# Turning the delta rule's values and queries on the vector engine instead of the tensor engine, in a two-layer hybrid decoder trunk

## The chip, the cores and the metric

The kernel runs on one core of a Trainium2 chip. A core has five engines with instruction streams of their own: the tensor engine (PE, with its weight loads shown apart as PEld), the vector engine (DVE), the scalar engine (ACT), GpSimd (POOL) and the sync engine (SP), which here issues every DMA. The engines meet through semaphores only, and each works through its own instructions in the order in which the program lists them. Compute reads and writes SBUF, 128 partitions wide; the tensor engine writes PSUM, eight banks of 128 x 512 float32. DRAM is reached by DMA.

The metric is the device time of one execution in microseconds (us), as the median of three runs. The profile is one further execution, with its own time.

## The reference

The trunk has two layers over a sequence of 2048 tokens of 1024 channels. Each layer projects its input to all heads at once, runs four heads of a gated delta rule beside four heads of gated linear attention (GLA), gates and mixes the heads, and adds the residual under a LayerNorm. Cut to the delta rule, which the change touches:

```python
dn_qkv = silu(causal_short_conv(concat([dn_q, dn_k, dn_v]), conv_w))   # 4 taps per channel
q = l2norm(cq) * 128 ** -0.5 ;  k = l2norm(ck) ;  v = cv               # per head of 128 channels
g = -exp(a_log) * softplus(dn_a + dt_bias) ;  beta = sigmoid(dn_b)
# per head:  S_t = a_t (I - b_t k_t k_t^T) S_{t-1} + b_t k_t v_t^T ,  o_t = S_t^T q_t    (a_t = exp g_t)
o_dn = head_rms_norm(o_dn, norm_g) * silu(dn_z)
y = concat([o_dn, o_gla]) @ w_out ;  x = layer_norm(alpha * x + y)
```

Everything is float32. The kernel does the delta rule in chunks of 128 tokens: within a chunk a triangular inverse, between chunks a 128 x 128 state S per head.

## The kernel before

**Tiling.** Each layer is done in two halves of 1024 tokens, so there are four passes, called halves below. A half is two blocks of 512 tokens, a block four chunks of 128. A projection of one head is a group of 24 matmuls into one PSUM bank (tag `pj`): the input `xt` and the weights are split into a high and a low part of a rounded float32 type (`xt`, `wh`, `wl`), and high x high, high x low and low x high are summed. Its output has channels on the partitions and the block's 512 tokens along the free axis.

**Where turns are needed.** The delta rule needs some tensors the other way round, with tokens on the partitions. The function `transpose4` makes four tensor-engine transposes of 128 x 128 into a bank with tag `tr` (the names `tr<-ident,...` in the profile, `ident` being the identity matrix). It is called three times per head and block: in `dn_keys`; in `dn_values`, where the convolved values are turned and then scaled per token by the vector engine straight out of PSUM; and in `dn_queries`, where the turned queries serve only the per-token sums of squares, which the scalar engine takes by `sumsq4`. GLA turns its keys the same way, and the very first input too. The layer's input and the attention output are already turned in another way (`turned`): the vector engine transposes 32 x 32 blocks in place (STREAM_TRANSPOSE), and the loads bring the blocks to their places.

**The recurrence.** `dn_rec` goes through the four chunks of a block. Each chunk is a chain over the engines: PE multiplies keys and queries by the state (`ch<-Sd,kq`), DVE forms the right-hand side `rr` from it and the scaled values `vb`, PE applies the inverse (`ch<-rr,m`), ACT or DVE scales that to `vn`, PE makes the state's update and the output (`ch<-vn,m`), DVE updates the state `Sd`. The turned values are first needed in `rr`; the queries' sums of squares only when the block's output is normalised.

**The inverse.** `dn_invert` sends small blocks to DRAM and back twice (`nd`, then `ud`), a round trip of the kind that the change adds; `dn_merge` puts the inverse together on PE.

**What sets the order.** A recorder (class `Recorder`) takes down all operations with their dependences, and a list scheduler with a table of costs chooses the order in which every engine's instructions are written; at the end one line (L433) emits them all, so every row of the profile carries that line, and groups are told apart by tile names. The scheduler takes the ready operation with the smallest key. The key is the operation's place in the program, less a lift. The text `PLAN` lists the stages of a half in program order, with a lift behind a plus sign: `q` and `w` are GLA's projections, `a` and `b` its two parts per pair of heads and block, `d` decays, `k`, `v`, `y` the delta rule's keys, values and queries of a head, `i` and `m` inverse and merge, `r` the recurrence of a head and block, `g` a gate's projection. Operations that two engines can do (`copy`, `scaled`, `subtract`, `product`) go to the one that the scheduler finds free sooner.

**Buffers.** Tiles are taken from a fixed number of slots per tag: three `tr` banks, twenty tiles of tag `m2`, five of `m4`, two raw weight tiles `wr`, three each of `wh` and `wl`. An operation that needs a slot waits until one is free.

Of the kernel before, what the change touches and what calls it, by code (L numbers as in the profile page):

```python
# [14 lines left out]
ALU = mybir.AluOpType  # L15
# [461 lines left out]
def _cost(o, outs, ins):  # L477
# [57 lines left out]
    else:  # L535
# [5 lines left out]
P = 128  # L541
# [3 lines left out]
NC = BLK // P  # L545
# [10 lines left out]

LAST = 1, 2, 3
FIRST = 300
PLAN = ("q0+50 w a00 d1 b00+50 a01 q1 d0+100 a10 b01 d2 k0 v0 b10+50 g4 a11 i0 b11+700 y0+100 k1+500 g5+200 m0 r00 k2 y1 "
        "r01 d3+200 i1 m1+50 v1 k3 g6 r10 y2 i2 m2+500 i3+150 v2+450 v3+100 r20 g7+400 m3+250 r11+950 r21 g0+100 y3+50 r30 r31")  # L560


@with_exitstack
def hymba_trunk(ctx: ExitStack, tc, x, w_in, conv_w, dn_a_log, dn_dt_bias, gla_gate_w2, gla_gate_b,
# [12 lines left out]
    def C(shape, name, dt=F32):  # L577
        return rec.sbuf(shape, name, dt)
# [4 lines left out]
    def small(w):  # L583
        return T([P, w], "s1")
# [21 lines left out]
    m0 = C([P, 32], "m0", U8)  # L606
# [60 lines left out]
    def bc(ap, n):  # L667
        return ap.unsqueeze(2).to_broadcast([ap.shape[0], ap.shape[1], n])
# [5 lines left out]
    subtract, product = partial(combine, ALU.subtract), partial(combine, ALU.mult)  # L674

    def copy(out, a, pool=False):
        calls = [("scalar", "copy", (out, a), {}), ("vector", "tensor_copy", (out, a), {})]
        if pool:
            calls.append(("gpsimd", "tensor_copy", (out, a), {}))
        rec.either(*calls)  # L680

    def scaled(out, a, by):
        rec.either(("scalar", "activation", (out, a, AF.Copy), dict(scale=by)),
                   ("vector", "tensor_scalar", (), dict(out=out, in0=a, scalar1=by, scalar2=None, op0=ALU.mult)))
# [51 lines left out]
    def proj_group(w, xtb):  # L736
        hi, lo = w
        xh, xl = xtb
        acc = PS([P, BLK], "pj")
        for k in range(KT):  # L740
            nc.tensor.matmul(acc, hi[:, k, :], xh[:, k, :], start=(k == 0), stop=False)
            nc.tensor.matmul(acc, hi[:, k, :], xl[:, k, :], start=False, stop=False)
        for k in range(KT):
            nc.tensor.matmul(acc, lo[:, k, :], xh[:, k, :], start=False, stop=(k == KT - 1))
        return acc
# [136 lines left out]
    def load_dec(decd, h, b):  # L882
        dec = T([P, NC, P], "m2")
        nc.sync.dma_start(dec, decd[h * NB + b].rearrange("p (c t) -> p c t", c=NC))
        return dec
# [197 lines left out]
    def conv_silu(acc, grp, tag):  # L1083
        raw = T([P, 515], "raw")
        nc.gpsimd.tensor_copy(raw[:, 0:3], halo[:, grp, :])
        copy(raw[:, 3:515], acc)
        nc.gpsimd.tensor_copy(halo[:, grp, :], raw[:, 512:515])
        y = T([P, BLK], tag)
        scaled(y, acc, cw[:, 36 + grp:37 + grp])
        for k in (2, 1, 0):  # L1090
            nc.vector.scalar_tensor_tensor(out=y, in0=raw[:, k:k + BLK], scalar=cw[:, 12 * k + grp:12 * k + grp + 1],
                                           in1=y, op0=ALU.mult, op1=ALU.add)
        nc.scalar.activation(y, y, AF.Silu)
        return y

    def transpose4(src):
        pt = PS([P, NC, P], "tr")
        for c in range(NC):
            nc.tensor.transpose(pt[:, c, :], src[:, c * P:(c + 1) * P], ident)
        return pt  # L1100

    def across(src):

        half = T([P, 4, NC, 32], "m2")
        nc.vector.transpose(half.pattern(0, [(32, NC), (P, 4), (1, 32)]), src.rearrange("p (c b t) -> p c b t", c=NC, b=4))
        d = DR([4, 32, 4, P], "tp")
        nc.sync.dma_start(d.rearrange("a i b e -> (a i) (b e)"), half.rearrange("p b c i -> p (b c i)"))
        t = T([P, 4, P], "m2")
        for a in range(4):
            nc.sync.dma_start(t[:, a, :], d[a].rearrange("t b e -> b t e"))  # L1110
        return t.pattern(0, [(32, NC), (P, 4), (1, 32)])

    def bc4(ap):
        return ap.unsqueeze(2).unsqueeze(3).to_broadcast([P, NC, 4, 32])

    def blocks(t):
        return t.rearrange("p c (a i) -> p c a i", a=4)

    def sumsq4(pt, dst):
        for c in range(NC):  # L1120
            o, i = T([P, P], "sq", BF16), pt[:, c]
            if len(i.dims) > 1:
                o = o.rearrange("p (a i) -> p a i", a=4)
            nc.scalar.activation(o, i, AF.Square, accum_out=dst[:, c:c + 1])
# [127 lines left out]

    def dn_values(l, h, b, w, xtb, st):
        k = st["b"][b]
        pt = transpose4(conv_silu(proj_group(w, xtb), 8 + h, "m2"))
        if b == 0:
            st["vb"] = T([P, NCH, P], "m4")
        nc.vector.tensor_tensor(out=st["vb"][:, b * NC:(b + 1) * NC, :], in0=pt, in1=bc(k["rk"], P), op=ALU.mult)

    def dn_queries(l, h, b, w, xtb, decd, st):  # L1260
        k = st["b"][b]
        dec = load_dec(decd, h, b)
        qT = conv_silu(proj_group(w, xtb), h, "kq")
        pa = PS([P, NC, P], "tr")
        for c in range(NC):
            cs = slice(c * P, (c + 1) * P)
            nc.tensor.matmul(pa[:, c, :], k["kT"][:, cs], qT[:, cs], start=True, stop=True)
        if b == 0:
            st["at"] = T([P, NCH, P], "m4")
        nc.vector.tensor_tensor(out=st["at"][:, b * NC:(b + 1) * NC, :], in0=pa, in1=dec, op=ALU.mult)  # L1270
        sq_ = small(NC)
        sumsq4(transpose4(qT), sq_)
        nc.vector.tensor_scalar(out=sq_, in0=sq_, scalar1=128.0 * EPS, scalar2=128.0 * EPS * EPS,
                                op0=ALU.mult, op1=ALU.add)
        k["qT"], k["sq"] = qT, sq_
# [121 lines left out]
    for l in range(depth):  # L1397
# [4 lines left out]
        for hf in range(n_half):  # L1402
# [72 lines left out]
            def values(h):  # L1475
                w = load_group(l, V0 + P * h)
                for b in range(NB):
                    dn_values(l, h, b, w, xt[b], dn[h])

            def queries(h):  # L1480
                w = load_group(l, Q0 + P * h)
                for b in range(NB):
                    dn_queries(l, h, b, w, xt[b], decd, dn[h])
# [3 lines left out]
                     "m": lambda h: dn_merge(dn[h]), "r": rec_block}  # L1487
            for step in PLAN.split():
                name, _, ahead = step.partition("+")
# [40 lines left out]
```

## Time and profile before

| | |
|---|---|
| three runs | 2093.4 us median (2091.4 to 2093.82) |
| the profiled execution | 2097.92 us |
| its span, first to last instruction | 2096.2 us, granted tensor clock 0.997 |
| PE busy | 2058.8 us, 98% |
| DVE busy | 1478.2 us, 71% |
| ACT busy | 1159.4 us, 55% |
| POOL busy | 504.9 us, 24% |
| DMA | 249.00 MB, mean 119 GB/s |
| STREAM_TRANSPOSE on DVE, 128 x 512 | 112 of 686 ns |
| `tr<-ident` turns on PE, 128 x 128 | 512 |

Rows of groups read: engine, operation, output<-inputs by tile name, shape, count | busy us, mean ns of one | idle time of the engine just before them, and what ended it. Matmuls overlap, and a row's duration is the time from start to end of one; what a matmul costs the engine is the distance to the next start. A float32 matmul of 128 columns shows as two records, a float32 transpose as one.

### The profile page before, as it was taken

To read this page: it belongs to the slowest core of one execution; us is meant where nothing else is said; L and a number is where in the kernel's file an instruction comes from. 1 tells how busy PE (TensorE), PEld (TensorE's weight loads), DVE (VectorE), ACT (ScalarE), POOL (GpSimd) and SP (SyncE) were. 2 spreads that over 40 slices of the span, in tenths; PEclk is the share of its full clock that TensorE was granted. 3 is DMA by queue.
4 is the path that set the end of the run, shared out by engine and by line. 5 is a ranking of instruction groups with operands and counts; after the bars stand their busy time and mean duration, and the time that the engine had idled before them with its cause. 6 is when DMAs were issued, how large, how long until landed. Compare 5 with 4: busy or idle time off the path is not lost.

```text
span 2096.2 us, 45723 instructions
## 1 busy us (share of the span) xinstructions
PE 2058.8 (98%) x16882; PEld 1742.3 (83%) x16882; DVE 1478.2 (71%) x3349; ACT 1159.4 (55%) x3284; POOL 504.9 (24%) x864
## 2 busy tenths in 40 slices
PE   7999999999999999999999999999999999999998
PEld 7888888888888887787888888878888888877877
DVE  4478787479657778757965777865795577886576
ACT  3677765532557775553266766555227576665520
POOL 3243211012234221111213322210131442211121
PEclk9999999999999999999999999999999999999999
DMA  4232433597223433359623333235962333333692
GB/s 142 74 99 81 126 89 80 144 228 207 72 72 103 113 89 79 94 157 242 177 72 82 99 97 104 76 87 173 235 187 59 90 95 100 93 78 85 176 224 71
DMA packets 334616, 249.00 MB, mean 119 GB/s; under 512 B 64756, under 2 KB 284216, under 8 KB 334392
## 3 DMA queue, kind: packets, MB, share of 16 engines
q1 hardware_dynamic: 334392, 246.08, 44.3%
q8 instruction: 133, 2.18, 0.5%
q14 instruction: 91, 0.75, 0.1%
HBM read 183.01 MB, written 62.98 MB: 117 GB/s over the span
## 4 chain that ended last, share of the span: by engine, by line
PE 86%; DMA 5%; DVE 4%; issue 2%; ACT 2%; POOL 1%; SPq 0%; DVEq 0%; ACTq 0%; POOLq 0%
PE pj L433 68%; PE ch L433 8%; PE tr L433 8%; PE mg L433 2%; DMA m<-zg 2%; DVE tmp L433 1%; DVE m L433 1%; DMA m<-in_w_out_dram 1%; DVE R L433 1%; ACT m L433 1%; DMA m<-xs 1%; SPq L433 0%; DMA m<-in_x_dram 0%; DMA U<-ud 0%; ACT wh L433 0%
## 5 line engine op out<-in xcount | busy, mean ns | idle before, releaser
L433 PE MATMUL pj<-xt,wh 128*128 128x512 f32 x4096 | 1068.2, 401 | 11.7 <-ACT wh L433 6.4
L433 PEld LDWEIGHTS pj<-xt,wh 128*128 128x128 f32 x4096 | 747.2, 189 | 160.8 <-ACT wh L433 8.6
L433 PE MATMUL pj<-xt,wl 128*128 128x512 f32 x2048 | 551.1, 399 | 0.0
L433 PEld LDWEIGHTS pj<-xt,wl 128*128 128x128 f32 x2048 | 373.8, 188 | 69.4 <-issue 0.2
L433 POOL TENSOR_TENSOR s<-s,mhalf 128x4 f32<-128x4 f32 (+2 forms) x80 | 95.5, 1194 | 440.6 <-DVE s L433 431.8
L433 PE MATMUL pj<-wh,xt 128*128 128x256 f32 (+1 forms) x1024 | 194.6, 289 | 1.9 <-ACT xt L433 0.9
L433 PEld LDWEIGHTS pj<-wh,xt 128*128 128x128 f32 x1024 | 162.0, 190 | 3.8 <-ACT xt L433 1.5
L433 ACT CAST wh<-wr 128x1024 fp32r<-128x1024 f32 (+2 forms) x116 | 117.5, 1019 | 83.3 <-PE pj L433 78.3
L433 DVE SCALAR_TENSOR_TENSOR kq<-raw,cw,kq 128x512 f32<-128x512 f32 x192 | 145.6, 759 | 14.6 <-ACT kq L433 9.6
L433 DVE TENSOR_TENSOR wl<-wr,wh 128x512 fp32r<-128x512 f32 (+2 forms) x173 | 122.5, 737 | 17.6 <-ACT wh L433 13.0
L433 PE MATMUL pj<-wl,xt 128*128 128x280 f32 (+1 forms) x512 | 130.6, 288 | 0.0
L433 ACT CAST wh<-m 128x1024 fp32r<-128x1024 f32 (+2 forms) x44 | 36.3, 829 | 155.3 <-DVE m L433 63.7
L433 DVE TENSOR_TENSOR m<-m,m 128x256 f32<-128x256 f32 (+1 forms) x209 | 89.6, 452 | 22.2 <-ACT m L433 8.3
L433 ACT COPY m<-m 64x256 f32<-64x256 f32 (+1 forms) x228 | 89.4, 412 | 18.4 <-DVE m L433 8.4
L433 PEld LDWEIGHTS pj<-wl,xt 128*128 128x128 f32 x512 | 97.6, 191 | 0.3
L433 POOL MEMSET m<- 128x512 f32 (+1 forms) x160 | 78.3, 507 | 52.5 <-PE tr L433 45.4
L433 DVE SCALAR_TENSOR_TENSOR Sd<-Sd,eg,ch 128x128 f32<-128x128 f32 x112 | 38.6, 345 | 71.6 <-PE ch L433 70.8
L433 PEld LDWEIGHTS ch<-Sd,kq 128*128 128x128 f32 x480 | 72.2, 190 | 13.0 <-DVE Sd L433 1.6
L433 PEld LDWEIGHTS ch<-vn,m 128*128 128x128 f32 x496 | 74.5, 191 | 10.3 <-ACT vn L433 0.9
L433 ACT ACTIVATE sq<-tr 128x128 bf16<-128x128 f32 x256 | 67.6, 276 | 22.5 <-PE tr L433 12.6
L433 POOL COPY halo<-raw 128x3 f32<-128x3 f32 x96 | 23.5, 245 | 234.7 <-ACT raw L433 187.9
L433 PE MATMUL ch<-vn,m 128*128 128x128 f32 x496 | 77.6, 276 | 0.4 <-ACT vn L433 0.4
(205 smaller groups left out, 3330.9 us busy)
## 6 DMA issues: line engine op xcount, KB each, us to landing
wr<-in_w_in_dram SPq DMA_DIRECT2D x312, 128.0 KB, 2.8
og<-m SPq DMA_DIRECT2D x64, 256.0 KB, 2.4
m<-decd SPq DMA_DIRECT2D x64, 256.0 KB, 3.5
zg<-m SPq DMA_DIRECT2D x64, 256.0 KB, 2.5
m<-in_w_out_dram SPq DMA_DIRECT2D x128, 128.0 KB, 3.9
m<-og SPq DMA_DIRECT2D x128, 128.0 KB, 4.5
m<-zg SPq DMA_DIRECT2D x128, 128.0 KB, 4.3
wr<-in_w_in_dram SPq DMA_DIRECT2D x26, 512.0 KB, 3.9
```

The costliest lines, as they stand in the source:

```text
L433: getattr(getattr(self.nc, o.eng), o.name)(*[real(a) for a in o.args], **{k: real(a) for k, a in o.kw.items()})
```

## The change

The two calls of `transpose4` in `dn_values` and `dn_queries` become calls of `across`, and the stage table is another one.

```diff
-PLAN = ("q0+50 w a00 d1 b00+50 a01 q1 d0+100 a10 b01 d2 k0 v0 b10+50 g4 a11 i0 b11+700 y0+100 k1+500 g5+200 m0 r00 k2 y1 "
-        "r01 d3+200 i1 m1+50 v1 k3 g6 r10 y2 i2 m2+500 i3+150 v2+450 v3+100 r20 g7+400 m3+250 r11+950 r21 g0+100 y3+50 r30 r31")
+PLAN = ("q0 w a00 d1 b00+50 a01 q1 d0 a10 b01 d2 k0 v0 b10+50 g4 a11 i0 b11+900 y0+100 k1+900 m0 g5+200 r00 y1 k2 "
+        "d3+800 i1 r01 m1+50 v1 r10 y2 i2 m2+600 r11+950 k3 g6 i3+250 m3+250 v2+450 r20+50 g7+400 v3+150 r21+50 g0 y3+200 r30 r31")
...
     def dn_values(l, h, b, w, xtb, st):
         k = st["b"][b]
-        pt = transpose4(conv_silu(proj_group(w, xtb), 8 + h, "m2"))
+        pt = across(conv_silu(proj_group(w, xtb), 8 + h, "m2"))
         if b == 0:
             st["vb"] = T([P, NCH, P], "m4")
-        nc.vector.tensor_tensor(out=st["vb"][:, b * NC:(b + 1) * NC, :], in0=pt, in1=bc(k["rk"], P), op=ALU.mult)
+        product(blocks(st["vb"][:, b * NC:(b + 1) * NC, :]), pt, bc4(k["rk"]))
...
         sq_ = small(NC)
-        sumsq4(transpose4(qT), sq_)
+        sumsq4(across(qT), sq_)
```

`across` stood in the file before and was called by nothing:

```python
    def across(src):
        half = T([P, 4, NC, 32], "m2")
        nc.vector.transpose(half.pattern(0, [(32, NC), (P, 4), (1, 32)]), src.rearrange("p (c b t) -> p c b t", c=NC, b=4))
        d = DR([4, 32, 4, P], "tp")
        nc.sync.dma_start(d.rearrange("a i b e -> (a i) (b e)"), half.rearrange("p b c i -> p (b c i)"))
        t = T([P, 4, P], "m2")
        for a in range(4):
            nc.sync.dma_start(t[:, a, :], d[a].rearrange("t b e -> b t e"))
        return t.pattern(0, [(32, NC), (P, 4), (1, 32)])
```

One vector instruction transposes the sixteen 32 x 32 blocks of all four chunks where they stand. One DMA writes the result to DRAM, 2 KB from each partition, and four DMAs read it back, each 128 runs of 512 bytes, so that the blocks change places. The result lies in SBUF, where the turned tensor lay in PSUM before: the values' scaling now reads two SBUF operands, and `product` lets the scheduler give it to DVE or POOL; the squares of the queries read SBUF. Eight DRAM buffers (tag `tp`) serve the trips in turn, and each call takes two more `m2` tiles and one `tr` bank less.

## The prediction

> **What bounds the kernel now.** I read the page's shares first, then the slices, then the chain that ended last.
>
> ```profile
> span 2096.2 us, 45723 instructions
> PE 2058.8 (98%) x16882; PEld 1742.3 (83%) x16882; DVE 1478.2 (71%) x3349; ACT 1159.4 (55%) x3284; POOL 504.9 (24%) x864
> ...
> PE   7999999999999999999999999999999999999998
> ...
> DMA packets 334616, 249.00 MB, mean 119 GB/s; under 512 B 64756, under 2 KB 284216, under 8 KB 334392
> ...
> PE 86%; DMA 5%; DVE 4%; issue 2%; ACT 2%; POOL 1%; SPq 0%; DVEq 0%; ACTq 0%; POOLq 0%
> ```
>
> PE is busy in every slice but the first and last, and makes 86% of the chain. A busy PE may still be waiting inside an instruction, so I went to the four stretches in which the delta rule runs, one per layer and half.
>
> ```profile
> 127.00:440.00 313.00, 313.00 (x2764) 262.44 (x2763) 227.82 (x576) 203.13 (x639) 66.84 (x125) 1.00 0.41 113
> 636.00:952.00 316.00, 313.23 (x2747) 262.05 (x2746) 227.47 (x573) 202.23 (x635) 72.28 (x129) 1.00 0.41 110
> 1154.00:1469.00 315.00, 310.97 (x2741) 258.70 (x2740) 227.76 (x582) 198.24 (x626) 68.30 (x125) 1.00 0.39 107
> 1671.00:1991.00 320.00, 315.10 (x2747) 263.32 (x2746) 228.68 (x573) 202.00 (x635) 71.06 (x126) 0.99 0.39 106
> sum 1264.00, PE 1252.30 PEld 1046.51 DVE 911.73 ACT 805.60 POOL 278.48; mean PE 313.07 PEld 261.63 DVE 227.93 ACT 201.40 POOL 69.62
> ```
>
> The columns are length, then busy time of PE, PEld, DVE, ACT and POOL, granted clock, DMA share, GB/s. PE idles 1264.0 - 1252.3 = 11.7 us in all four; DVE is busy 911.7 / 1264 = 72%, the DMA engines about 40%. Here PE's own issue rate sets the time, so what leaves PE should leave the span.
>
> **What leaves PE.** The timeline of the first stretch shows a turn inside a run of projection matmuls, and one behind the attention product.
>
> ```profile
> 163.78 1.07 PE L433 MATMUL pj<-xt,wl 128*128 128x512 f32 x4
> 164.70 0.60 PE L433 MATMUL tr<-ident,m 128*128 128x128 f32 x4
> 165.05 0.72 PE L433 MATMUL pj<-xt,wl 128*128 128x512 f32 x2
> ...
> 204.96 1.98 PE L433 MATMUL pj<-xt,wl 128*128 128x512 f32 x8
> 206.77 0.38 PE L433 MATMUL tr<-kq,kq 128*128 128x128 f32 x2
> 206.99 0.60 PE L433 MATMUL tr<-ident,kq 128*128 128x128 f32 x4
> 207.35 0.48 PE L433 MATMUL pj<-xt,wh 128*128 128x512 f32 x1
> ```
>
> First column: start. Four turns inside projections hold PE from 164.70 to 165.05, 0.35 us; neighbours lose nothing visible (the four matmuls before take 164.70 - 163.78 = 0.92 us, 0.23 each). Behind tr<-kq,kq the group takes 206.99 to 207.35, 0.36 us, but without it the last float32 pass would hand over to a projection sooner: its two passes take 0.22 us, 0.11 each, whereas the last of four turns hands over after 0.36 - 3 x 0.11 = 0.03. Removing such a group therefore saves up to 4 x 0.11 = 0.44 us.
>
> The groups of PE bear out the counts:
>
> ```profile
> L433 PE MATMUL tr<-ident,m 128*128 128x128 f32 x256 | 40.1, 287 | 9.3 <-DMA m<-in_x_dram 8.9 <-DVE xt L433 0.4
> L433 PE MATMUL tr<-ident,kq 128*128 128x128 f32 x256 | 38.9, 273 | 0.0
> ```
>
> Two calls x 4 heads x 2 blocks x 4 halves = 64 groups of four go, half from each row; keys, gated attention and the first input keep the other 256 turns. The same place in the built program, PE, the query product of the first head's first block (kq_168 is the query, pj_159 and pj_160 the projections around it); before:
>
> ```order
> L433 MATMUL pj_159<-xt_148,wl_144 128x512 x8
> L433 MATMUL tr_157<-kq_168,kq_175 128x128
> L433 MATMUL tr_155<-ident_63,kq_168 128x128 x4
> L433 MATMUL pj_160<-xt_149,wh_140 128x512
> L433 MATMUL pj_160<-xt_148,wl_143 128x512 x8
> ```
>
> and now:
>
> ```order
> L433 MATMUL pj_159<-xt_148,wl_144 128x512 x8
> L433 MATMUL tr_155<-kq_168,kq_175 128x128 x2
> L433 MATMUL pj_160<-xt_148,wh_140 128x512
> L433 MATMUL pj_160<-xt_149,wh_140 128x512
> L433 MATMUL pj_160<-xt_148,wl_143 128x512 x8
> ```
>
> The turns are gone, the rest stands. Value groups mostly lie among projections, query groups behind the product: 32 x 0.35 + 32 x 0.44 = 11.2 + 14.1 = **25.3 us**, between 64 x 0.35 = 22.4 and 64 x 0.44 = 28.2.
>
> **What comes in its place.** These groups give the prices (count | busy us, mean ns | idle before).
>
> ```profile
> L433 DVE STREAM_TRANSPOSE kq<-m 128x512 f32<-128x512 f32 x112 | 72.8, 686 | 6.1 <-DMA m<-og 5.8 <-DMA m<-xs 0.2
> L433 DVE TENSOR_TENSOR m<-tr,s 128x512 f32<-128x512 f32 x32 | 22.0, 688 | 5.2 <-PE tr L433 4.3 <-POOL m L433 0.5
> L433 DVE TENSOR_TENSOR m<-kq,m 128x512 f32<-128x512 f32 x49 | 33.3, 699 | 15.3 <-DMA m<-zg 10.6 <-ACT m L433 3.7 <-DMA zg<-m 1.0
> L433 POOL TENSOR_TENSOR m<-kq,m 128x512 f32<-128x512 f32 x31 | 46.2, 1502 | 110.9 <-DMA m<-zg 46.3 <-DVE kq L433 32.5 <-PE pj L433 13.2
> L433 DVE TENSOR_TENSOR wl<-wr,wh 128x512 fp32r<-128x512 f32 x158 | 106.0, 702 | 7.3 <-ACT wh L433 6.1 <-DMA decd<-m 0.5
> L433 ACT ACTIVATE sq<-tr 128x128 bf16<-128x128 f32 x256 | 67.6, 276 | 22.5 <-PE tr L433 12.6 <-DVE m L433 9.5
> L433 ACT ACTIVATE sq<-m 128x128 bf16<-128x128 f32 x128 | 39.3, 307 | 66.7 <-DVE m L433 60.7 <-DVE s L433 3.5 <-DVE R L433 1.6
> ```
>
> DVE gets 64 block turns of 512 columns: 64 x 0.686 = 43.9 us. Its 32 products out of PSUM (22.0 us) become products out of SBUF, 28 on DVE (19.6 us by the 699 ns row), 4 on POOL (6.0 us). By the built program's counts the new order also hands 16 weight differences of 512 columns from DVE to POOL, 11.2 us less on DVE (POOL is at 278.5 / 1264 = 22%). DVE's net is 43.9 - 22.0 + 19.6 - 11.2 = +30.3 us, less some copies and scalings that ACT takes; over four stretches that lifts 72% to at most (911.7 + 30.3) / 1264 = 75%. The 128 query squares on ACT read SBUF instead of PSUM: 128 x (307 - 276) = 4.0 us on an engine at 64%. The projections that PE runs meanwhile hide both, so I cost them at nothing; without that cover they would be 34.3 us.
>
> [...]
>
> The transfers add 64 writes of 256 KB and 256 reads of 64 KB on SP, 33.6 MB beside 249; at 40% DMA share that is hidden. What is late is the round trip. Its likeness is the inverse's trip nd:
>
> ```profile
> 229.53 0.37 SPq L433 DMA_DIRECT2D nd<-T  x1
> 230.00 0.53 SPq L433 DMA_DIRECT2D zg<-m  x1
> 232.36 0.38 SPq L433 DMA_DIRECT2D wr<-in_w_in_dram  x1
> 232.80 1.03 SPq L433 DMA_DIRECT2D m<-nd  x2
> ...
> DMA to landing us min/median/max: 2.2/2.7/8.3
> ...
> L433 SPq DMA_DIRECT2D nd<-T x16: 360/388/398, 172.2 to 1886.1; - x16
> ...
> SPq L433 <- DMA nd<-T: 23.4, 12, 3.5
> SPq L433 <- DVE wl L433: 389.4, 90, 27.9
> DVE V L433 <- DMA m<-nd: 3.1, 5, 0.9
> ```
>
> Write to first read 3.3 us, three more issues at about 0.5, landing 2.7: some 7.5 us. The wait falls on whoever reads the result in line. DVE, second value block of the third head (m_11_124 the convolved values, m_10_123 the turned ones, m_4_154 the scaled values); before:
>
> ```order
> L433 SCALAR_TENSOR_TENSOR rr_216<-ch_163,eg_104,m_4_154 128x128
> L433 TENSOR_TENSOR wl_143<-wr_138,wh_140 128x512
> L433 STREAM_TRANSPOSE T_0_204<-U_0_212 128x256
> L433 COPY m_3_129<-T_0_204 32x8x32 x2
> L433 TENSOR_TENSOR m_0_150<-tr_156,s_6_188 128x512
> ```
>
> and now:
>
> ```order
> L433 STREAM_TRANSPOSE m_16_126<-m_11_124 128x4x4x32
> L433 COPY Nd_201<-m_4_120 32x128 x2
> L433 TENSOR_TENSOR wl_145<-wr_138,wh_141 128x512
> L433 STREAM_TRANSPOSE T_0_212<-Nd_201 128x256
> L433 TENSOR_SCALAR vn_222<-ch_163,s_14_196 128x128
> L433 TENSOR_SCALAR m_7_136<-m_7_136,gg_90 128x512
> L433 TENSOR_TENSOR wl_143<-wr_139,wh_140 128x512 x2
> L433 SCALAR_TENSOR_TENSOR rr_224<-ch_163,eg_104,m_4_154 128x128
> L433 COPY V_215<-m_0_150 128x128
> L433 TENSOR_TENSOR m_4_154<-m_10_123,s_4_187 128x512
> ```
>
> The product now stands ten instructions behind its turn, the shortest distance of the 28; it was fed by PSUM. Three differences alone are 2.1 us; with the rest I estimate some 5 us against 7.5, so DVE may stand 2.5 us there, with V's chain queued behind it. The likeness says less: V waited for nd in 5 of 16 places, 3.1 us in all, 0.2 each. At 0.2 the 64 trips cost 12 us of DVE and ACT idling, off PE's path. I take 0 for PE, since values are needed only when their head's recurrence starts.
>
> **The order.** The table adds no instruction; it puts the fourth head's keys and a gate's projection (k3, g6) behind the second head's two recurrence blocks, and v3 behind the third's first, with the weight and decay loads that they issue on SP. So the projections that cover a recurrence's waits are others, and PE's idle places move. It can at best remove the 11.7 us above, and I allow as much the other way; nothing in the trace says which, so 0.
>
> **Sum.** The profiled execution took 2097.92 us around its span of 2096.2; less 25.3 is 2072.6. It lay 4.5 above the runs' median of 2093.4, from which I count: 2093.4 - 25.3 = **2068**. Range: low 2093.4 - 28.2 - 11.7 = 2053; high 2093.4 - 22.4 + 11.7 = 2083, a microsecond added for ACT.
>
> **Rivals.**
> *Vector waits reach PE (slower).* DVE is in line: a product that stands for its trip holds up the recurrence's rr or S behind it. PE has four projections between those steps:
>
> ```profile
> 306.84 0.61 PE L433 MATMUL ch<-Sd,kq 128*128 128x128 f32 x4
> 307.20 1.16 PE L433 MATMUL pj<-xt,wh 128*128 128x512 f32 x4
> 308.21 0.38 PE L433 MATMUL ch<-rr,m 128*128 128x128 f32 x2
> ...
> PE ch L433 <- DVE rr L433: 2.9, 3, 1.9
> ```
>
> That is 308.21 - 307.20 = 1.0 us of cover. With 2.5 us at all 28 products, 28 x 1.5 = 42 us reach PE: 2068 + 42 = **2110**. It decides from 25.3 / 28 = 0.9 us beyond cover per product. For it: that estimate of 2.5. Against: 2.9 us of waiting for rr in the whole trace, and V's 0.2.
> [...]
> *SP makes weights late.* Each trip's reads wait at SP's head for the write, 23.4 / 12 = 2 us by the row, with weight loads behind. Were 13 of the 64 to delay a load by 1 us that PE feels: **2081**. Against: loads already stand 389.4 us for a free buffer, so they run ahead.
> *The turns were free*: PE would wait anyway for the recurrence, and nothing changes, **2093**. Against: 11.7 us idle in 1264.
>
> **Chances.** Forecast 0.72, weights late 0.12, Vector waits 0.09, free turns 0.07. A change within 0.2% (4.2 us) can't be told from none. Faster: 0.72 + 0.12 + 0.01 = 0.85; same: 0.06 + 0.01 = 0.07; slower 0.08. The range 2053 to 2084 leaves out the last two cases and the forecast's tails.
>
> **What would show it.** Right: the groups tr<-ident,kq and tr<-ident,m at 128 each, PE's busy time lower by about 25 us and still 98%, DVE between 1490 and 1510 us, its waits on the trips' reads under 15 us, PE's wait for rr under 5 us. Wrong: PE under 97% in the stretches, long waits of PE for DVE rr or Sd (the second case) or for ACT wh (the third); a block turn far over 686 ns; or a PE as long as before.

## The result, and the profile after

The changed kernel took 2120.7 us in the median (2117.1 to 2127.4), the kernel before 2093.4: a ratio of **1.0133, 95% interval 1.0119 to 1.0146**, so 27 us slower where 25 us faster had been forecast. Its profiled execution took 2127.4 us. The page's head, with the clock of the whole execution below it:

```profile
span 2125.7 us, 45829 instructions
PE 2055.1 (97%) x16626; PEld 1726.5 (81%) x16626; DVE 1485.4 (70%) x3339; ACT 1175.7 (55%) x3328; POOL 536.2 (25%) x894
...
DMA packets 377627, 282.57 MB, mean 133 GB/s; under 512 B 66804, under 2 KB 319032, under 8 KB 377400
```
```profile
core 0: 2125.7 us, clock 0.989
```

The 256 transposes are gone (16882 to 16626 records), and yet PE is busy only 3.7 us less. Three parts explain the span. PE stands idle for 2125.7 - 2055.1 = 70.6 us, before for 37.4: +33.2. The clock that was missing is (1 - 0.989) x 2125.7 = 23.4 us, before (1 - 0.997) x 2096.2 = 6.3: +17.1. What is left, busy time without the clock's share, went from 2052.5 to 2031.7: -20.8. The sum is +29.5, the difference of the two spans. So the gain was there, and more than twice as much was lost in idling and in a lower clock.

The four stretches of the delta rule (columns as in the prediction: length, busy time of PE, PEld, DVE, ACT, POOL, granted clock, DMA share, GB/s):

```profile
126.00:447.00 321.00, 308.67 (x2673) 255.17 (x2672) 226.80 (x573) 204.23 (x644) 73.11 (x131) 0.98 0.47 131
655.00:966.00 311.00, 306.93 (x2680) 253.95 (x2679) 230.31 (x576) 204.64 (x641) 74.44 (x133) 1.00 0.48 134
1172.00:1500.00 328.00, 311.10 (x2667) 256.64 (x2667) 225.19 (x556) 206.16 (x654) 77.86 (x135) 0.97 0.45 126
1707.00:2021.00 314.00, 308.62 (x2683) 255.60 (x2682) 232.07 (x580) 204.10 (x639) 75.21 (x132) 0.99 0.47 133
sum 1274.00, PE 1235.31 PEld 1021.35 DVE 914.37 ACT 819.13 POOL 300.62; mean PE 308.83 PEld 255.34 DVE 228.59 ACT 204.78 POOL 75.16
```

PE's idle time in them grew from 11.7 to 1274.0 - 1235.3 = 38.7 us. Whom PE waited for, and who waited for the trips (total us, times, longest):

```profile
PE ch L433 <- DVE Sd L433: 11.2, 9, 2.3
...
PE pj L433 <- DVE m L433: 6.9, 7, 3.3
PE pj L433 <- ACT wh L433: 6.6, 8, 2.3
...
PE ch L433 <- DVE rr L433: 3.8, 3, 3.2
```
```profile
DVE m L433 <- DMA m<-tp: 25.1, 17, 3.5
DVE V L433 <- DMA m<-nd: 20.1, 5, 6.4
...
ACT sq L433 <- DMA m<-tp: 13.4, 10, 3.2
...
POOL m L433 <- DMA m<-tp: 18.2, 4, 12.8
...
SPq L433 <- DMA tp<-m: 72.3, 37, 3.7
```

PE waits for the state `Sd` 11.2 us (0.4 before) and for `rr` hardly more than before (3.8 against 2.9); for weights on ACT no longer than before (6.6 against 6.4). Three engines wait 56.7 us for the new trips, and the inverse's old trip `nd` is now waited for 20.1 us instead of 3.1, though nothing in it was changed. (For this kernel the profile pairs a wait with the last transfer issued on the semaphore that ended it, so the name of a transfer is inferred.) SP's queue is held at its head for 72.3 us by reads whose write hasn't landed.

The second value block of the first head shows it in one place: SP's queue, then the rows of DVE, ACT, POOL and PE that follow from it (start, length, what; in brackets the idle time before):

```profile
171.02 0.43 SPq L433 DMA_DIRECT2D tp<-m  x1
...
172.02 0.42 SPq L433 DMA_DIRECT2D nd<-T  x1
175.00 2.34 SPq L433 DMA_DIRECT2D m<-tp  x4
177.43 1.90 SPq L433 DMA_DIRECT2D m<-nd  x4
```
```profile
182.42 0.69 DVE L433 TENSOR_TENSOR m<-m,s 128x512 f32<-128x512 f32 x1 [3.50 <-DMA m<-tp]
```
```profile
183.41 0.41 ACT L433 COPY m<-m 64x256 f32<-64x256 f32 x1 [4.45 <-DVE s L433]
```
```profile
183.47 1.80 POOL L433 TENSOR_TENSOR s<-s,mhalf 128x8 f32<-128x8 f32 x1 [6.36 <-DVE s L433]
```
```profile
186.69 0.46 PE L433 MATMUL tr<-m,m 128*32 128x32 f32 x32 [1.28 <-POOL m L433]
187.08 1.66 PE L433 MATMUL pj<-xt,wh 128*128 128x512 f32 x6
190.76 3.69 PE L433 MATMUL pj<-xt,wh 128*128 128x512 f32 x8 [2.03 <-ACT kq L433]
```

From the write's issue at 171.02 to the product at 182.42 the trip lasts 11.4 us. DVE stands 3.5 us for it, ACT and POOL stand for DVE, and PE, four microseconds on, for them: 3.3 us in two pauses. In the 31 places where an engine waited for a trip it lasted 6.6 to 12.6 us from the write's issue, 9.7 in the median.

### The profile page after: what moved, and what is told of

Same layout as the page of the kernel before. It is cut to its first block, busy times and chain, and to the rows that moved or that the text cites. A ratio compares the mean times of both kernels' runs of the same rounds, so it can differ in the third digit from the quotient of the medians.

```text
span 2125.7 us, 45829 instructions
## 1 busy us (share of the span) xinstructions
PE 2055.1 (97%) x16626; PEld 1726.5 (81%) x16626; DVE 1485.4 (70%) x3339; ACT 1175.7 (55%) x3328; POOL 536.2 (25%) x894
## 5 line engine op out<-in xcount | busy, mean ns | idle before, releaser
L433 PEld LDWEIGHTS pj<-xt,wh 128*128 128x128 f32 x4096 | 754.9, 191 | 176.7 <-ACT wh L433 14.2
L433 DVE TENSOR_TENSOR wl<-wr,wh 128x512 fp32r<-128x512 f32 (+2 forms) x156 | 115.0, 764 | 30.9 <-ACT wh L433 24.1
L433 ACT ACTIVATE sq<-m 128x128 bf16<-128x128 f32 x256 | 77.2, 304 | 90.5 <-DVE m L433 71.1
L433 POOL TENSOR_TENSOR wl<-wr,wh 128x512 fp32r<-128x512 f32 (+1 forms) x56 | 77.6, 1390 | 84.3 <-PE pj L433 36.9
L433 PE MATMUL ch<-Sd,kq 128*128 128x128 f32 x480 | 79.5, 282 | 11.5 <-DVE Sd L433 11.2
L433 PEld LDWEIGHTS ch<-vn,m 128*128 128x128 f32 x496 | 74.1, 192 | 17.1 <-ACT vn L433 4.6
```

The source lines that it names most:

```text
L433: getattr(getattr(self.nc, o.eng), o.name)(*[real(a) for a in o.args], **{k: real(a) for k, a in o.kw.items()})
```

## The experiments

Each kernel was timed beside the kernel before on the same chip, which took 2092.0 to 2093.6 us in the median. Ratios are to that, with their 95% interval. The diffs show the deciding lines only, in places shortened; a label behind a line names its run.

### Is it the new table?

e1 is the change with the table of before; e2 is the kernel before, its turns on PE, with the table of the change (the same two lines the other way round).

```diff
-PLAN = ("q0 w a00 d1 b00+50 a01 q1 d0 a10 b01 d2 k0 v0 b10+50 g4 a11 i0 b11+900 y0+100 k1+900 m0 g5+200 r00 y1 k2 "
+PLAN = ("q0+50 w a00 d1 b00+50 a01 q1 d0+100 a10 b01 d2 k0 v0 b10+50 g4 a11 i0 b11+700 y0+100 k1+500 g5+200 m0 r00 k2 y1 "
...
```

> The changed kernel with the stage table of before: the turns go through DRAM, the order is the planner's answer to the old table. Theory 1, the trips' waits: the changed kernel's reader of a turned tensor stands in line on DVE, ACT or POOL until a trip of about 11 us has landed (I had reckoned 7.5), and PE runs dry; the old table has the same trips, so 2095 to 2125 us. Theory 2, the new table: the order of stages costs the time and the turns give what was forecast, so about 2068 us (2060 to 2080). Theory 3, SP's queue: the 320 added DMAs hold up the other loads on SP; as theory 1, 2095 to 2125 us.

> The kernel before with the stage table of the change: turns on PE, no trips. Theories 1 and 3: the table is not the cause, 2085 to 2100 us. Theory 2: the table itself costs some 50 us, 2130 to 2150 us.

Measured: the change with the old table 2152.0 us (ratio 1.0289, 1.0271 to 1.0307), the old turns with the new table 2090.0 (0.9989, 0.9980 to 0.9998). The table isn't the cause: alone it is worth 2 us, and without it the change would be 31 us slower still, which is more than any of the three theories expected.

### What do the trips cost?

Three runs keep the written order of the change, and in all three the readers take a constant tile in place of the turned blocks. e3 and e10 leave out the trip's DMAs as well, e10 the block turns too; e4 keeps both.

```diff
             for o in order:
+                if o.eng == "sync" and any(v.buf.tag == "tp" for v in sum(_operands(o), [])):      # e3, e10
+                    continue
+                if o.eng == "vector" and any(id(v.buf) in halves for v in _operands(o)[0]):        # e10
+                    continue
+                o.args, o.kw = tuple(still(o, a) for a in o.args), {k: still(o, a) for k, a in o.kw.items()}
```

> The changed kernel in its own written order, without its 320 trip DMAs; the readers of the turned tensors (the values' scaling, the queries' squares) read a constant tile of the same shape instead, so values and query norms are left out of the computation. The block turns on DVE stay. Theories 1 and 3: the added waits go, 2062 to 2080 us. Theory 2: the order is unchanged, so 2110 to 2122 us.

> The changed kernel in its own written order with all its trip DMAs, but nobody reads what they bring: the readers of the turned tensors read a constant tile of the same shape (values and query norms are left out of the computation). It takes the waits for the trips away and keeps SP's load. Theory 1: 2065 to 2085 us. Theory 2: 2110 to 2122 us. Theory 3: SP's queue is as full as before, 2105 to 2122 us. Between 2085 and 2105 us both the waits and the queue have a share, which the difference from the run without trips then gives.

> As the run without trip transfers (2083.8 us), and the 64 block turns of the vector engine (0.65 us each, 42 us of it) are left out too, so that nothing of the turn is left but its readers (values and query norms are left out). If the vector engine's added work kept PE from its gain, this run nears the 25.3 us of the forecast below before: 2066 to 2075. If PE, with its transposes gone, only runs into the other waits sooner (the output's and the inverse's trips, casts of weights), it stays at 2079 to 2085.

Measured: without trips 2083.8 us (0.9958, 0.9946 to 0.9971), with the trips' transfers but nobody waiting for them 2107.6 (1.0074, 1.0050 to 1.0098), without trips and turns 2082.8 (0.9953, 0.9938 to 0.9968). So of the 37 us between the change and the run without trips, 13 go to waits for the turned blocks, and 24 to the transfers themselves, whose blocks nobody waits for; e4's interval leaves 5 us either way in this split. The 64 block turns on DVE cost 1 us, which is within the noise: there the forecast, that the projections hide them, held. The run without trips took 4 us more than the 2062 to 2080 expected.

The run without trips also tells why even a free trip doesn't give 25 us. Its head and that of the old turns with the same table:

```profile
span 2081.3 us, 45188 instructions
PE 2036.2 (98%) x16626; PEld 1718.3 (83%) x16626; DVE 1485.0 (71%) x3339; ACT 1175.3 (56%) x3328; POOL 532.6 (26%) x894
```
```profile
span 2086.7 us, 45640 instructions
PE 2055.2 (98%) x16882; PEld 1737.8 (83%) x16882; DVE 1462.4 (70%) x3330; ACT 1156.1 (55%) x3287; POOL 515.0 (25%) x880
```

Their clocks were 0.995 and 0.999. With (1 - clock) x span taken off, PE's work is 2025.8 against 2053.1: 27.3 us less, a little over the 25.3 forecast. But PE idles 45.1 us instead of 31.5, and the clock loses 8.3 more; 5.4 us of the span are left. A PE that arrives sooner can stand at other trips, which in this order end no sooner. Its longest pause after the start, on PE, and what DVE had stood for shortly before (`og` is the trip of the attention output, in the kernel before as well):

```profile
987.72 1.52 PE L447 MATMUL pj<-xt,wh 128*128 128x512 f32 x5 [3.21 <-DVE m L447]
```
```profile
979.37 1.31 DVE L447 STREAM_TRANSPOSE kq<-m 128x512 f32<-128x512 f32 x2 [2.44 <-DMA m<-og]
```

From there DVE works without a pause; only at 986.90 does it come to the instruction that empties the PSUM bank (`m<-m,pj`, 0.68 us), and PE's projection starts when that is done. The two runs share the table but not the written order (that of e3 was laid out for trips), so how much of the idle time is a PE that comes too soon and how much is the order wasn't separated.

### Is it SP's held queue, or readers that were written too early?

e5 is e4 with reads that take their bytes from the input, so that they don't wait for their write. e8 is the change, but the planner (the list scheduler) is told that a trip lasts 3 us longer.

```diff
+                if o.eng == "sync" and any(v.buf.tag == "tp" for v in _operands(o)[1]):            # e5
+                    src = o.args[1]
+                    o.args = (o.args[0], bass.AP(x.tensor, x.offset + src.off, [tuple(d) for d in src.dims]))
...
                 o.end = dma_free + (900.0 if o.bufs[0].space == "dram" else 1000.0)
+                if any(v.buf.tag == "tp" for v in _operands(o)[1]):                                # e8
+                    o.end += 3000.0
```

> The run with all the round trips' transfers and no engine waiting for them took 2107.6 us, the one without the transfers 2083.8. Here the transfers stay, in the same written order and as many (64 writes, 256 reads of 64 KB), and the turned blocks are still not used (a constant tile stands in for them, so values and query norms are left out); but each read takes its bytes from the input in DRAM, so that it no longer waits at the head of SP's queue for its write to land (72.7 us in 39 waits). If the held queue is what the transfers cost, the time falls to 2084 to 2092 us, as without transfers. If it is their issues and their bytes on the DMA engines, it stays at 2102 to 2110.

> The changed kernel with one number of the planner altered: when it sets the order, a read of the trip ends 3 us later, so that a trip is reckoned at about 11 us instead of 8.0 (where an engine was seen to wait for one, it took 6.6 to 12.6 us, median 9.7). All work stays. If readers written too early are the harm (Vector, ACT and POOL standing at the head of their queues), most of the 13 us between the change and the run without such waits comes back: 2100 to 2112 us, and the waits for the trip, 56.7 us on three engines, fall under 20. If the held SP queue and the transfers are the harm, it stays at 2112 to 2130.

Measured: e5 2095.7 us (1.0013, 1.0001 to 1.0025), between the two expectations: the held head is worth 12 us of the 24, and 12 stay with transfers that hold nothing, again give or take 5. e8 2116.9 (1.0129, 1.0104 to 1.0153). Its waits for the trip, total us, times, longest:

```profile
DVE m L435 <- DMA m<-tp: 4.8, 4, 1.7
...
ACT sq L435 <- DMA m<-tp: 5.5, 5, 1.7
...
POOL m L435 <- DMA m<-tp: 9.8, 3, 4.5
...
SPq L435 <- DMA tp<-m: 77.1, 38, 3.5
```

The waits for the trip fell from 56.7 to 20.1 us as asked, and the time by 4, which is within the two intervals. Readers written too early are not the lever: in the new order others wait longer, DVE's `V` for `nd` 25.7 us instead of 20.1 and PE for `Sd` 13.7 instead of 11.2.

### Values or queries?

```diff
-        pt = across(conv_silu(proj_group(w, xtb), 8 + h, "m2"))                                    # e6
+        pt = transpose4(conv_silu(proj_group(w, xtb), 8 + h, "m2"))
...
-        sumsq4(across(qT), sq_)                                                                    # e7
+        sumsq4(transpose4(qT), sq_)
```

> Only the 32 query groups take the DRAM trip; the values are turned on PE as before. Table of the change; the order comes out anew. If the trips cost by their number (SP's queue, transfers), half of them cost half: between 2090.0 (the old turns with this table) and 2120.7, so 2100 to 2110 us. If the harm is the vector engine standing before the values' product, with the recurrence's rr and Sd behind it, the values carry it and this run is at 2086 to 2096, while the run with the values alone stays at 2110 to 2120.

> Only the 32 value groups take the DRAM trip; the queries' copies for the norm are turned on PE as before. Table of the change, order anew. If the trips cost by their number: 2100 to 2110 us. If the harm lies with the values' product on the vector engine: 2110 to 2120. If it lies with the queries, whose four squares on ACT wait and hold casts of the weights (13.4 us of such waits after the change): 2088 to 2098.

Measured: queries alone 2089.1 us (0.9983, 0.9973 to 0.9993), no more than e2 without any trip (2090.0), values alone 2110.1 (1.0097, 1.0062 to 1.0131), at the seam of two expectations. The number of trips is the same, so it isn't the number alone. In these two runs the values carry the harm, as one would expect of tensors that the recurrence needs in time; but the planner set the order anew for each, so the order's share isn't separated. In the run with values alone DVE waits 36.8 us for its trips in 15 places, and PE 8.9 us for `Sd` and 5.1 for `rr`.

### The shape of the trip

e9 is e5 with every read cut to 16 of its 128 columns. e11 cuts the whole trip the other way: four writes of 64 KB, one read of 256 KB. e12 does so for queries alone, e13 with the old table.

```diff
-        d = DR([4, 32, 4, P], "tp")
-        nc.sync.dma_start(d.rearrange("a i b e -> (a i) (b e)"), half.rearrange("p b c i -> p (b c i)"))
+        d = DR([4, 4, 32, P], "tp")
+        for a in range(4):
+            nc.sync.dma_start(d[a].rearrange("b t e -> t b e"), half[32 * a:32 * a + 32].rearrange("p b c i -> p b (c i)"))
         t = T([P, 4, P], "m2")
-        for a in range(4):
-            nc.sync.dma_start(t[:, a, :], d[a].rearrange("t b e -> b t e"))
+        nc.sync.dma_start(t, d.rearrange("a b t e -> (b t) a e"))
```

> As the run whose reads don't wait for their writes (2095.7 us), with every read cut to its first 16 of 128 columns: as many transfers, issues and rows, an eighth of the reads' bytes (values and query norms are left out, as there). Without any trip transfers it was 2083.8. If the bytes on the DMA engines make the 12 us, it falls to 2084 to 2088. If the 320 issues on SP and the rows' packets make them, it stays at 2093 to 2098.

> The changed kernel with its trip cut the other way: four writes of 64 KB and one read of 256 KB. One read instead of four is queued behind the landing of the write, with the same bytes and as many issues; the order comes out anew. If SP, held by reads and then busy 2.3 us with issuing four of them, is the larger share, the trip is 1.5 to 2 us shorter and the time 2100 to 2112 us. If it is the number of transfers and bytes, 2113 to 2128.

> Queries alone through DRAM (2089.1 us with one write and four reads; before 2092.7 beside it), by four writes and one read. If issuing the reads behind the landing costs there too, 2080 to 2087 us, which would beat both kernels; if the queries' trips cost nothing as they are, 2087 to 2092.

> Four writes and one read for values and queries, with the table of before (one write and four reads with that table: 2152.0 us; four writes and one read with the new table: 2079.7). If the shape of the trip makes the 41 us between the change and the run with one read, it makes some 40 here too: 2105 to 2120 us. If the new run was merely a fortunate order, this one is no better than 2140.

Measured: e9 2086.2 us (0.9962, 0.9949 to 0.9975), so an eighth of the bytes with as many issues takes back 9.5 of the 12 us. e11 **2079.7 (0.9935, 0.9918 to 0.9951)**, far under what either theory expected, and faster than both kernels. e12 2086.5 (0.9967, 0.9956 to 0.9979). e13 2097.9 (1.0020, 1.0011 to 1.0029), 54 us under the same table with the change's trip and better than the 40 expected; but with that table the new trip doesn't win against the kernel before. All bytes travel in e11 as before, in as many transfers.

### The shape, or the order that comes with it?

The planner sets all engines' order anew for e11. e14 keeps the order of the change and puts the new shape into its places; e15 is the opposite, the order of e11 with the shape of the change. e16 is e5 with a single read of 256 KB.

```diff
+                if o.eng == "sync" and any(v.buf.tag == "tp" for v in _operands(o)[0]):            # e14
...
+                    for a in range(4):
+                        self.nc.sync.dma_start(d[a].rearrange("b t e -> t b e").real(),
+                                               half.pattern(0, [(P, 4), (1, P)])[32 * a:32 * a + 32].real())
+                    continue
+                if o.eng == "sync" and any(v.buf.tag == "tp" for v in _operands(o)[1]):
+                    reads[id(o.args[1].buf)] = reads.get(id(o.args[1].buf), 0) + 1
+                    if reads[id(o.args[1].buf)] == 4:
...
+                        self.nc.sync.dma_start(t.real(), d.rearrange("a b t e -> (b t) a e").real())
+                    continue
```

> The written order of the change (2120.7 us) with nothing moved: at the place of each write stand four writes of 64 KB, at the place of the last of four reads one read of 256 KB. If the shape alone decides, the time falls to the neighbourhood of the run with one read, 2080 to 2095. If the order that came out with it decides, it stays at 2112 to 2125.

> The other way round: the written order of the run with four writes and one read (2079.7 us), with one write at the place of the last of four and four reads at the place of the one. If the shape alone decides: 2110 to 2125. If the order decides: 2080 to 2092.

> The run whose reads don't wait for their writes (2095.7 us; with an eighth of the bytes 2086.2; without any transfer 2083.8), with one read of 256 KB in place of four of 64 KB: the same bytes and rows, 192 issues fewer; values and query norms are left out as there. If the bytes make the 12 us, it stays at 2093 to 2098. If it is the number of reads that are under way at once or are issued, 2083 to 2089.

Measured:

| written order | one write, four reads | four writes, one read |
|---|---|---|
| of the change | 2120.7 | 2090.4 (e14: 0.9987, 0.9974 to 1.0001) |
| of e11 | 2129.3 (e15: 1.0174, 1.0157 to 1.0191) | 2079.7 |

The shape is worth 30 us in one order and 50 in the other. The order is worth about 10, in opposite directions: that of e11 is the better one for its own trip and the worse one for the change's. e15 lies 4 us above the range that was expected if the shape decides. e16: 2084.3 (0.9952, 0.9937 to 0.9967), no more than without any transfer. The place quoted above, in e14, SP and then DVE:

```profile
170.47 2.01 SPq L437 DMA_DIRECT2D tp<-m  x4
...
173.86 0.36 SPq L446 DMA_DIRECT2D m<-tp  x1
175.76 2.00 SPq L448 DMA_DIRECT2D m<-nd  x4
```
```profile
178.00 0.68 DVE L448 TENSOR_TENSOR m<-m,s 128x512 f32<-128x512 f32 x1
```

The same product in the same order starts at 178.00 without a wait, 7.5 us behind the first write.

### Number of reads, or their rows?

Four reads and one read differ in number, and in how they walk through DRAM. In the change a read's source has the dimensions 4 x 32 x 128 (`t b e -> b t e`): the outermost counts 4. In e16 and e14 it counts 128. e17 is e5, and e18 is e14, with four reads of 64 KB that go through DRAM row by row, 128 x 128.

```diff
-   bass.AP(x.tensor, x.offset + src.off, [tuple(d) for d in src.dims])                             # e17
+   bass.AP(x.tensor, x.offset + src.off, [(P, P), (1, P)])
...
+   o.args = (o.args[0], View(o.args[1].buf, None, None, o.args[1].off, [(P, P), (1, P)], F32))     # e18
```

> The run with four free reads of 64 KB (2095.7 us) against the one with a single free read of 256 KB (2084.3) differs in the number of reads and in the order of their rows: the four step through DRAM by 2 KB and back (32 rows of 512 B, four times), the single one goes straight on. Here are four reads of 64 KB that go straight on; values and query norms are left out as there. If the number of reads costs the 11 us, this stays at 2092 to 2098; if the order of the rows, it is at 2083 to 2088.

> The written order of the change with four writes and four reads of 64 KB, the reads' rows straight on in DRAM (the writes now do the turning): one write and four turning reads took 2120.7 us, four writes and one read 2090.4. If the number of reads behind the landing costs, 2112 to 2130, for 192 issues more than the change has; if it was the order of the reads' rows, 2088 to 2102.

Measured: e17 2085.4 us (0.9964, 0.9953 to 0.9975) against 2095.7, e18 2095.5 (1.0015, 1.0003 to 1.0027) against the change's 2120.7, with 192 more transfers than the change has. **It is how the read walks**, not how many there are; going from four reads to one (e14) is worth 5 us more.

What is different about these reads can be counted in the trace. A transfer raises its semaphore in steps, sixteen for nearly all of them: 1427 transfers and 22776 steps in the profile before, 56 short of sixteen each, and the same 56 are missing in every run without such reads. After the change it is 1747 transfers and 25080 steps, 2872 short: 2816 more, which is 256 x 11. In e18 with 1939 transfers it is 56 again; in e6, with half as many such reads, 1408 = 128 x 11 more. So each of the change's reads is seen in five steps. The profile's list of DMA issues shows the gap as well: it gives a median time to landing only where the steps come out on the semaphore that the transfers share, and after the change no row of it has one, the trip's or any other's. In e18 (count, KB each, us to landing):

```profile
tp<-m SPq DMA_DIRECT2D x256, 64.0 KB, 1.8
m<-tp SPq DMA_DIRECT2D x256, 64.0 KB, 2.5
```

In prices of the trace: packets of 512 bytes took 27 ns in the median, before and after the change, in e5 and in e16 alike. After the change 73 to 78 rows of 512 bytes start in each half microsecond from 1.5 to 3.5 us behind a trip's first read, in the mean over 56 trips (rows of other transfers are counted in). At 27 ns a row that is, by estimate, four rows at a time (75 x 27 / 500 = 4.05), and the 4 x 128 rows of a trip's four reads take 128 x 27 ns = 3.5 us. In e18 up to 155 rows start in half a microsecond, in e14 up to 204: eight and eleven at a time by the same estimate. So all four reads of a trip together go four rows at a time, though the single row is no slower. From the end of the last read's issue to its waiting reader it took 4.0 us in the median after the change and 2.1 in e18. e9 fits: packets of 64 bytes took 11 ns, by the same estimate 1.4 us for 128. That other transfers stand behind these rows, and that e5 pays for this without waiting for a trip, is the author's estimate; what was measured is DVE's wait for the inverse's `nd` trip: 19.1 us in e5, 5.7 in e17 and 2.2 in e16. With the trip itself waited for it was 20.1 us after the change, and still 16.0 in e18, 9.1 in e14, 6.5 in e11. Why it is four isn't shown: the records don't name the engine of a packet, and an outermost dimension of 8 wasn't tried.

## Why the prediction was wrong

The ladder in the written order of the change, from the medians: 2120.7 as it is; 2095.5 with reads in row order (-25.2); 2090.4 with one read (-5.1); 2083.8 without trips (-6.6); 2082.8 without block turns (-1.0). The forecast was 2068: 37 us of the error are the trip, and 16 were missing even without it.

**What leaves PE: right.** 25.3 us, 22.4 to 28.2: PE's work fell by 27.3 us between the two runs with one table. The change's own 20.8 is less; where the other 6 went is open, since a busy record may hold waiting (a matmul of `pj<-xt,wh` shows as 389 ns in the median, and the next starts after 227).

**DVE's and ACT's work at nothing: right** on DVE, 1 us by e10; ACT's squares were in every run. Its rows after the change, and the squares':

```profile
L433 DVE STREAM_TRANSPOSE m<-kq 128x512 f32<-128x512 f32 x32 | 22.6, 706 | 4.9 <-ACT kq L433 4.4
L433 DVE STREAM_TRANSPOSE m<-m 128x512 f32<-128x512 f32 x32 | 22.6, 706 | 4.8 <-ACT m L433 4.6
...
L433 DVE TENSOR_TENSOR m<-m,s 128x512 f32<-128x512 f32 x28 | 20.4, 728 | 33.8 <-DMA m<-tp 25.1 <-DMA wr<-in_w_in_dram 8.2 <-DMA zg<-m 0.4
...
L433 ACT ACTIVATE sq<-m 128x128 bf16<-128x128 f32 x256 | 77.2, 304 | 90.5 <-DVE m L433 71.1 <-DMA m<-tp 13.4 <-DVE s L433 3.6
```

The prices were 706 ns for 686, 728 for 699, 304 for 307. DVE's total rose by 7 us instead of 30, while POOL's rose by 31.3 and ACT's by 16.3. The mean of 728 ns hides one place: of the 28 products out of SBUF 27 took 694 ns at most, and the one that began while POOL worked on two SBUF operands took 1784, with 1.23 us of POOL's 1.44 beside it:

```profile
1406.32 1.44 POOL L433 TENSOR_TENSOR wl<-wr,wh 128x512 fp32r<-128x512 f32 x1
```
```profile
1406.53 1.78 DVE L433 TENSOR_TENSOR m<-m,s 128x512 f32<-128x512 f32 x1
```

The row `m<-kq,m`, which has two SBUF inputs as well, shows the same: without a POOL operation on SBUF beside them these products took 694 ns at most, with one up to 1391. So DVE can lose time beside POOL here, but of the new products it met one of 28, 1784 - 694 ns = 1.1 us in all.

**The trip: the step that failed.** "Write to first read 3.3 us, three more issues at about 0.5, landing 2.7: some 7.5 us", "at 0.2 the 64 trips cost 12 us of DVE and ACT idling, off PE's path", "I take 0 for PE". The likeness with `nd` was of the wrong kind. Its reads, like nearly all transfers, raise their semaphore in sixteen steps; the trip's reads, with 4 outermost, are seen in five. The trip lasted 9.7 us in the median where it was waited for, and its waits were 56.7 us on three engines against 12. The zero for PE is the term: in the change's order the trips cost 2120.7 - 2083.8 = 37 us, some 13 through waits for the blocks, 12 through SP's held head, 12 through transfers that nobody waits for. The sentence "at 40% DMA share that is hidden" is part of it: a mean share says nothing of reads whose rows go, by estimate, four at a time. How the reads walk wasn't weighed at all.

**The idle time of PE stays: wrong, and a second loss of 16 to 22 us.** Even without trips PE, 27.3 us shorter, gives only 5.4 of it to the span; the prediction put more idling at 0 in its sum, with 11.7 for the table in its range, and had no term for the clock. The rival "the turns were free" was nearer than its chance of 0.07: in this order PE waits for the most part of what it saves. In e11's order less so:

```profile
span 2079.2 us, 45688 instructions
PE 2034.5 (98%) x16626; PEld 1712.6 (82%) x16626; DVE 1496.9 (72%) x3351; ACT 1175.3 (57%) x3325; POOL 522.4 (25%) x885
...
DVE m L433 <- DMA m<-tp: 11.7, 10, 2.5
...
SPq L433 <- DMA tp<-m: 41.6, 49, 4.4
```

There, at a clock of 0.997, PE's work is 24.2 us lower than before and its idle time 7.3 higher: 17 us of the span are won, 13.6 by the medians. This is what the forecast described, at half to two thirds of its size.

**The order at 0: right** for the table alone (-2 us). But with the change's trip the two tables lie 31 us apart (2152.0 and 2120.7), and with one read 18 (2097.9 and 2079.7): with trips the order matters, and more so with slow ones.

**The slower rival** ended on the right side and near the size (2110), with its place half right: PE waits for DVE, above all for `Sd`, 11.2 us, not for `rr`. That the size came near is luck: it reckoned 42 us for the 28 products alone, where all waits for turned blocks came to 13; the larger part, 24 us through the queue and the transfers themselves, was no part of it. **Weights late** named SP's head rightly (72.3 us held) and the victims wrongly: not the weights (6.6 us against 6.4), but other trips.

## What to carry to other kernels

When a DMA is costed by another one's row, compare the access patterns first, the outermost count of both sides above all: here reads with 4 outermost started 73 to 78 rows in half a microsecond and reads with 128 outermost up to 155 or 204, and no mean share of DMA shows that. Let the write do the turning where its outermost dimension is larger, here 32 instead of 4: the same bytes in as many transfers, and 30 to 50 us. And work that is taken from the engine that sets the pace pays only as far as the next wait. Run the change once with the new cost taken out (here without the trips) to see what there is to win.

## What the runs showed of the hardware

**The clock fell behind short pauses.** Windows of the changed kernel around the place shown above (columns as before; the clock stands behind POOL's count):

```profile
180.00:186.00 6.00, 5.41 (x116) 4.26 (x114) 2.84 (x9) 2.26 (x6) 2.52 (x3) 1.00 0.83 177
186.00:190.76 4.76, 2.04 (x38) 1.40 (x39) 3.98 (x18) 3.88 (x11) 2.52 (x8) 1.00 0.41 116
190.76:194.17 3.41, 3.41 (x8) 2.69 (x9) 3.34 (x11) 1.16 (x4) 0.36 (x2) 0.51 0.59 153
194.17:200.00 5.83, 5.83 (x157) 4.73 (x156) 3.53 (x13) 1.61 (x4) 0.19 (x1) 1.00 0.07 22
```

PE was busy for 2.04 of 4.76 us, with two pauses of 1.3 and 2.0 us, and then ran 3.41 us at half clock: the eight matmuls there took 3.69 us, where eight take 1.98 in the rows of the prediction. So by estimate this pause of 2 us cost another 1.7, half of 3.41. Twelve such windows of 3.41 or 6.83 us lie in the changed kernel, two in the kernel before. Each of the twelve begins at most 2.3 us behind a pause of PE of 0.8 to 3.3 us, and in the 3.41 us before it PE was busy for 10 to 66%; not every pause brought one (one of 2.0 us at 1235.9 didn't).

**A read's walk shows in its issue, too.** SP took 0.51 us (median) to issue a 64 KB read with 4 outermost (after the change), 0.38 for one with 128 outermost (e18), and 0.38 for 256 KB in one read (e14).
